# One column unit turned by transposing DMA, and one product's split in halves, in a Trainium2 kernel of 7803 matmuls

## The chip, the cores and the metric

The kernel runs on one core of one Trainium2 chip. A core has a matmul engine (TensorE, PE in the profile), three engines that work on vectors and elements (VectorE or DVE, ScalarE or ACT, GpSimd or POOL), an engine that here only issues transfers (SyncE or SP), and 16 DMA engines that carry the transfers. Each engine runs its own instructions in their order, and waits on semaphores for the others.

The metric is the device time of one execution in microseconds (us). Times are medians over runs. The profile shows one execution.

## The reference

One decoder layer on 256 tokens of width 2048, everything in float32: a feed-forward block, a token mixer of two branches, a second feed-forward block, and a last normalisation.

```python
def swiglu_ffn(x, w_gate, w_up, w_down):
    return (jax.nn.silu(x @ w_gate) * (x @ w_up)) @ w_down

x = x + 0.5 * swiglu_ffn(rms_norm(x, ffn1_norm), ffn1_w_gate, ffn1_w_up, ffn1_w_down)
z = rms_norm(x, mix_norm) @ w_in
...
x = x + y @ w_out
x = x + 0.5 * swiglu_ffn(rms_norm(x, ffn2_norm), ffn2_w_gate, ffn2_w_up, ffn2_w_down)
return rms_norm(x, final_norm)
```

Gate and up weights are 2048 x 5632, down weights 5632 x 2048. The change touches the first feed-forward block at its start, and the gate products of both blocks; the mixer (the lines left out) is not touched.

## The kernel before

**Numbers in two parts.** A float32 operand is split in two for TensorE: `hi`, which ACT makes as a copy rounded to the type fp32r, and `lo`, the remainder that DVE subtracts out. A product of two such operands is three matmuls: high by high, low of the tokens by high of the weights, high of the tokens by low of the weights. `multiply` (L231) issues the two terms with the weights' high part first, then the one with their low part; so `hi` is wanted first and `lo` eight matmuls per target bank later (two targets: sixteen). The tokens are the stationary operand, the weights stream in blocks of 128 x 512.

**Blocks of weights.** A block is one *unit* of four 128-row pieces and 512 columns, 1 MB, loaded by SP at L165 into one of three rotating buffers `raw` (or, for two special blocks of `seven`, into one of two buffers `kept`). A rotating buffer is loaded again only when all readers of its last content are done. ACT and DVE split each block, TensorE multiplies it. Everything is traced by a helper (L43), so that almost all instructions have this line; rows are told apart by the names of the tiles. A tile scheduler decides the order on each engine from the written order and its own model, except where instructions are kept in program order (`Engine.pinned`, `keep_in_program_order`).

**Seven products for eight.** `seven` (L405) computes two column blocks of gate, up or down weights at a time. On the first two row units (0 and 1) it takes the 2 x 2 blocks w11, w12, w21, w22 by a scheme with seven products in place of eight, in which sums of weights are multiplied by sums of tokens; units 2 and 3 (b2, b3 for the second column block, a2, a3 for the first) are multiplied the usual way. The order in the program is: product 0 (w11), product 4 (w12 - w11), b2, **product 5** (w22 less the last sum; the third product), b3, product 6 (w22 - w12), product 2 (w22), a2, product 3 (w21 less product 5's sum), a3, product 1 (w21). The names in rows are `hi_g_p`, `lo_g_p` for parts of products and `hi_g_x`, `lo_g_x` for usual blocks, `raw_g` for loaded blocks and the sums, which are made in place: w11 and then the sums of products 4, 5 and 3 stand in one buffer, w12 and then the sum of product 6 in another. With buffer numbers, `raw_g_2_00` is w11's, `_01` w12's, `_11` w22's, `_10` w21's, `_21` and `_31` b2's and b3's, `_20` and `_30` a2's and a3's. SP loads w11, w12, b2, w22, b3, a2, w21, a3 in this order; w21 goes into the rotating buffer that held b3, whose last reader is the DVE operation `lo_g_x` of b3.

The flag `order` is set for the third and fifth of the five gate calls of each feed-forward block: four calls in all, called gate blocks here. In these, the low halves of product 4 and the sum of product 6 keep their program order. In all calls the sum and the parts of product 4 are made in halves of two pieces each; product 5 has one full sum over 128 x 2048, two casts and one full low part.

**The opening.** `begin` starts the first feed-forward block while its inputs arrive. It is pinned to program order. The tokens, as loaded in `xres`, lie with tokens across the partitions and must be turned for TensorE, unit by unit. Unit u is first scaled by the tokens' factors (`tokens`: two ACT operations into `n`, one for each half of the tokens), then eight transposes on TensorE write it into four banks `pt` (`turned_tokens`), then ACT writes the high part (`high`: four operations that scale by the gain) and DVE the low part (`low`: four). For unit 3 the transposes are issued in the middle of the up product of unit 2. Between its low parts and the product stand, on ACT and DVE, the sums of tokens for `seven` (`steps`).

**Turning by DMA.** Elsewhere the kernel turns tiles without TensorE: `part` (L203) copies a 128 x 512 tile on ACT into a half of `pair`, with the two 16-bit halves of each float32 apart, and SP issues one transposing DMA (L208, 8 blocks of 128 x 128 16-bit numbers) back into the tile; `join` (L211) copies the turned halves on ACT into `pair` again, as float32.

Of the kernel before, what the change touches and what calls it, by code (L numbers as in the profile page):

```python
# [12 lines left out]
U16 = mybir.dt.uint16  # L13
AF = mybir.ActivationFunctionType
ALU = mybir.AluOpType
# [34 lines left out]
def hybrid_block(ctx: ExitStack, tc: tile.TileContext, a: dict, out: bass.AP):  # L50
# [35 lines left out]
    def f32(ap):  # L86
        return ap.bitcast(F32)
# [123 lines left out]
    def join(two, turned):  # L211
        tc.keep_in_program_order(act.copy(two.bitcast(U16).rearrange(mixed, b=2), turned.rearrange(flat, b=2)))
        return quad(two)
# [17 lines left out]
    def multiply(targets, blk, apart=False, middle=None):  # L231


        more = dict(skip_group_check=True) if apart else {}
        for ps, st, begin, _ in targets:
            for j in range(UK):
                pe.matmul(ps, st[j][0], blk[j][0], start=begin and j == 0, stop=False, **more)
                pe.matmul(ps, st[j][1], blk[j][0], start=False, stop=False, **more)
        if middle:
            middle()  # L240
        for ps, st, _, end in targets:
            for j in range(UK):
                pe.matmul(ps, st[j][0], blk[j][1], start=False, stop=end and j == UK - 1, **more)
        if len(targets) == NT:
            onward()
# [159 lines left out]
    def seven(w, rows, cols, sf, xs, name, keep, done, between=None, ready=None, whole=True, order=False):  # L405


        a, c, e, d = (bank(f"ps_{name}_{n}") for n in "aced")

        def get(u, n, kept=False):  # L410
            src = w[u * UK * P : (u + 1) * UK * P, cols[n] : cols[n] + CW]
            return load(src, f"{name}_{u}{n}", kept=kept)

        (r0, r1), two = rows, len(xs) > 1
        w11, first = ready or (get(r0, 0, True), None)
        w12 = get(r0, 1, True)
        b2, w22 = get(xs[0][0], 1), get(r1, 1)
        b3 = get(xs[1][0], 1) if two else None
        a2, w21 = get(xs[0][0], 0), get(r1, 0)
        a3 = get(xs[1][0], 0) if two else None  # L420

        def snap(ps, n):
            s = keep(f"{n}_{name}")
            act.copy(s, ps)
            return s

        def product_of(i, raw, ps, begin=False, end=True, blk=None):
            multiply([(ps, sf[i], begin, end)], blk or parts_of(raw, f"{name}_p{i}"), True)

        def usual(i, raw, n, *targets):  # L430

            blk = parts_of(raw, f"{name}_x{i}{n}")
            multiply([(ps, stationary(xs[i][1], t), b, z) for ps, t, b, z in targets], blk, True)

        product_of(0, w11, a, True, blk=first)
        s1 = None if whole else snap(a, "s1")
        if whole:
            act.copy(d, a)
        hi, lo, blk = splits_of(f"{name}_p4")
        for i in (0, 2):  # L440
            o = slice(i, i + 2)
            dve.tensor_tensor(w11[:, o], w12[:, o], w11[:, o], op=ALU.subtract)
            act.copy(hi[:, o], w11[:, o])
        for i in (0, 2):
            o = slice(i, i + 2)
            ins = dve.tensor_tensor(lo[:, o], w11[:, o], f32(hi[:, o]), op=ALU.subtract)
            if order:
                tc.keep_in_program_order(ins)
        product_of(4, w11, c, True, blk=blk)
        s5 = snap(c, "s5")  # L450
        if between:
            between(0)
        usual(0, b2, 1, (e, 1, True, not two), (c, 0, False, False))
        if between:
            between(1)
        dve.tensor_tensor(w11, w22, w11, op=ALU.subtract)
        product_of(5, w11, a)
        u2 = snap(a, "u2")
        if between:
            between(2)  # L460
        if two:
            usual(1, b3, 1, (e, 1, False, True), (c, 0, False, False))
        ins = dve.tensor_tensor(w12, w22, w12, op=ALU.subtract)
        if order:
            tc.keep_in_program_order(ins)
        product_of(6, w12, a)
        u3 = snap(a, "u3")
        done(1, 1, e, [u3, s5])
        product_of(2, w22, c)
        done(0, 1, c, [u2])  # L470
        usual(0, a2, 0, (d, 0, not whole, False), (a, 1, False, False))
        dve.tensor_tensor(w11, w21, w11, op=ALU.subtract)
        product_of(3, w11, a, end=not two)
        if two:
            usual(1, a3, 0, (a, 1, False, True), (d, 0, False, False))
        done(1, 0, a, [])
        product_of(1, w21, d)
        done(0, 0, d, [] if whole else [s1])

    def ffn(tag, norm, after, opening=False):  # L480
        with (
# [73 lines left out]
            def begin():  # L555
# [28 lines left out]
                def tokens(u):  # L584
                    n = [keep(f"n{tag}_{u}_{t}") for t in range(NT)]
                    for t in range(NT):
                        act.activation(n[t], xres[:, t, u * CW : (u + 1) * CW], AF.Copy, scale=norm.r[:, t : t + 1])
                    return n

                def turned_tokens(u, n):  # L590
                    pts = []
                    for j in range(UK):
                        pt = bank(f"pt{tag}_{u}_{j}")[:, :S]
                        for t in range(NT):
                            pe.transpose(pt[:, t * P : (t + 1) * P], n[t][:, j * P : (j + 1) * P], ident)
                        pts.append(pt)
                    return pts

                def high(u, pts):
                    for j, pt in enumerate(pts):  # L600
                        act.activation(units[u][:, j, :S], pt, AF.Copy, scale=gain[:, UK * u + j : UK * u + j + 1])

                def low(u, pts):
                    for j, pt in enumerate(pts):
                        g = gain[:, UK * u + j : UK * u + j + 1]
                        hi, lo = units[u][:, j, :S], units[u][:, j, S:]
                        dve.scalar_tensor_tensor(lo, pt, g, f32(hi), op0=ALU.mult, op1=ALU.subtract)

                def targets(banks, u, y):
                    return [(banks[t], stationary(y, t), u == 0, u in (0, 3)) for t in range(NT)]  # L610
# [52 lines left out]
                low(2, pts2)  # L663
                dve.tensor_tensor(lo, rg, f32(hi), op=ALU.subtract)
                raw["g", 3] = first_columns("g", 3)
                n3, pts3 = tokens(3), []
                multiply(targets(gps, 2, units[2]), blk, True)
                steps = []
                sums(steps)
                blk = parts("u", 2)  # L670
                raw["u", 3] = first_columns("u", 3)
                multiply(targets(ups, 2, units[2]), blk, True, middle=lambda: pts3.extend(turned_tokens(3, n3)))
                blk = parts("g", 3)
                steps[0]()
                high(3, pts3)
                low(3, pts3)
                steps[1]()
                multiply(targets(gps, 3, units[3]), blk, True)
                blk = parts("u", 3)
# [503 lines left out]
```

## Time and profile before

| | us |
|---|---|
| median of 3 runs | 1713.93 |
| lowest and highest run | 1713.70, 1714.16 |
| profiled execution | 1712.3 |
| its span, first to last instruction | 1710.3 |

Core 0 had a granted clock of 0.999 of full speed over the profiled execution. The span is what the profile divides into; the 2.0 us between it and the execution's time lie outside the first and the last instruction. A row of the timeline begins with its start and its length in us, then engine, line and operation, the output and the inputs, and the count of like instructions that it groups; a bracket gives the time for which the engine had been idle, and what released it. The start of a matmul row is what counts, since matmuls are pipelined and the length of a row is more than its share of the engine. DVE and ACT also let the next instruction begin a little before the end of the last.

### The profile page before, as it was taken

To read this page: it belongs to the slowest core of one execution; us is meant where nothing else is said; L and a number is where in the kernel's file an instruction comes from. 1 tells how busy PE (TensorE), PEld (TensorE's weight loads), DVE (VectorE), ACT (ScalarE), POOL (GpSimd) and SP (SyncE) were. 2 spreads that over 40 slices of the span, in tenths; PEclk is the share of its full clock that TensorE was granted. 3 is DMA by queue.
4 is the path that set the end of the run, shared out by engine and by line. 5 is a ranking of instruction groups with operands and counts; after the bars stand their busy time and mean duration, and the time that the engine had idled before them with its cause. 6 is when DMAs were issued, how large, how long until landed. Compare 5 with 4: busy or idle time off the path is not lost.

```text
span 1710.3 us, 20226 instructions
## 1 busy us (share of the span) xinstructions
PE 1693.9 (99%) x7803; PEld 1412.4 (83%) x7803; DVE 1480.0 (87%) x1297; ACT 1169.9 (68%) x1489; POOL 6.9 (0%) x32
## 2 busy tenths in 40 slices
PE   8999999999999999999999999999999999999997
PEld 6888888888888888888888888888888888888886
DVE  7998988979889879787986679979989888889786
ACT  6767667776567678775655777676667765677864
POOL 1000000000000000000000000000000000000000
PEclk9999999999999999999999999999999999999999
DMA  8666567575567685855555685685666656576753
GB/s 300 206 221 198 197 221 221 190 257 206 184 208 210 225 267 143 244 172 194 174 194 174 220 271 167 205 257 194 226 201 217 223 191 221 197 215 203 249 194 123
DMA packets 235168, 358.43 MB, mean 210 GB/s; under 512 B 66884, under 2 KB 69312, under 8 KB 234944
## 3 DMA queue, kind: packets, MB, share of 16 engines
q1 hardware_dynamic: 234608, 356.03, 64.7%
q8 instruction: 61, 1.00, 0.2%
q10 hardware_dynamic: 144, 1.05, 0.2%
q14 instruction: 35, 0.29, 0.1%
q0 software_dynamic: 320, 0.07, 0.0%
HBM read 339.82 MB, written 2.10 MB: 200 GB/s over the span
## 4 chain that ended last, share of the span: by engine, by line
PE 92%; ACT 3%; DVE 2%; DMA 1%; issue 1%; SPq 0%; DVEq 0%; ACTq 0%
PE ps_d L43 14%; PE ps_in L43 13%; PE ps_g_a L43 9%; PE ps_u_a L43 8%; PE ps_u_c L43 6%; PE ps_d_a L43 5%; PE ps_o L43 5%; PE ps_g_c L43 5%; PE ps_g_d L43 5%; PE ps_d_c L43 3%; PE ps_u_d L43 3%; PE ps_u_e L43 3%; PE ps_g_e L43 3%; PE ps_d_d L43 3%; PE ps_u L43 2%; PE ps_g L43 2%
## 5 line engine op out<-in xcount | busy, mean ns | idle before, releaser
L43 ACT CAST hi_u_p<-raw_u 128x1024 fp32r<-128x1024 f32 x140 | 141.5, 1047 | 52.5 <-DVE raw_u L43 24.7
L43 ACT CAST hi_g_p<-raw_g 128x1024 fp32r<-128x1024 f32 x132 | 133.8, 1047 | 57.6 <-DVE raw_g L43 30.2
L43 DVE TENSOR_TENSOR lo_u_p<-raw_u,hi_u_p 128x2048 fp32r<-128x2048 f32 (+1 forms) x80 | 159.9, 2018 | 14.4 <-ACT hi_u_p L43 13.8
L43 DVE TENSOR_TENSOR lo_g_p<-raw_g,hi_g_p 128x2048 fp32r<-128x2048 f32 (+1 forms) x75 | 151.6, 2030 | 18.7 <-ACT hi_g_p L43 17.9
L43 PE MATMUL ps_d<-hi_d,h 128*128 128x512 f32 x704 | 167.0, 389 | 0.0
L43 PEld LDWEIGHTS ps_d<-hi_d,h 128*128 128x128 f32 x704 | 132.2, 188 | 27.4
L43 PE MATMUL ps_in<-xT_nm,hi_in 128*128 128x512 f32 x640 | 153.1, 391 | 0.0
L43 PEld LDWEIGHTS ps_in<-xT_nm,hi_in 128*128 128x128 f32 x640 | 117.5, 188 | 23.0 <-ACT tha L43 0.3
L43 ACT CAST hi_d_p<-raw_d 128x1024 fp32r<-128x1024 f32 x84 | 86.1, 1048 | 65.7 <-DVE raw_d L43 34.2
L43 DVE TENSOR_TENSOR lo_d<-raw_d,hi_d 128x2048 fp32r<-128x2048 f32 x44 | 100.2, 2289 | 34.7 <-ACT hi_d L43 34.5
L43 ACT CAST hi_in<-raw_in 128x1024 fp32r<-128x1024 f32 x80 | 80.1, 1046 | 59.6 <-PE ps_in L43 46.2
L43 DVE TENSOR_TENSOR lo_in<-raw_in,hi_in 128x2048 fp32r<-128x2048 f32 x40 | 91.3, 2284 | 33.9 <-ACT hi_in L43 33.6
L43 ACT CAST hi_u_x<-raw_u 128x1024 fp32r<-128x1024 f32 x80 | 81.3, 1047 | 37.1 <-PE ps_u_c L43 25.9
L43 DVE TENSOR_TENSOR lo_d_p<-raw_d,hi_d_p 128x2048 fp32r<-128x2048 f32 (+1 forms) x48 | 96.4, 2019 | 7.2 <-ACT hi_d_p L43 6.8
L43 DVE TENSOR_TENSOR raw_u<-raw_u,raw_u 128x2048 f32<-128x2048 f32 (+1 forms) x50 | 92.3, 1862 | 11.2 <-DMA raw_u<-in_ffn_w_up_dram 10.6
L43 ACT CAST hi_d<-raw_d 128x1024 fp32r<-128x1024 f32 x88 | 88.8, 1046 | 18.0 <-PE ps_d_d L43 7.6
L43 DVE TENSOR_TENSOR lo_g_x<-raw_g,hi_g_x 128x2048 fp32r<-128x2048 f32 x40 | 91.4, 2286 | 7.5 <-ACT hi_g_x L43 7.5
L43 ACT CAST hi_g_x<-raw_g 128x1024 fp32r<-128x1024 f32 x80 | 81.2, 1046 | 20.4 <-PE ps_g_c L43 8.6
L43 DVE TENSOR_TENSOR lo_u_x<-raw_u,hi_u_x 128x2048 fp32r<-128x2048 f32 x40 | 91.3, 2283 | 1.2 <-ACT hi_u_x L43 1.1
L43 DVE TENSOR_TENSOR raw_g<-raw_g,raw_g 128x2048 f32<-128x2048 f32 (+1 forms) x46 | 84.9, 1867 | 5.4 <-DMA raw_g<-in_ffn_w_gate_dram 4.8
L43 PE MATMUL ps_d<-lo_d,h 128*128 128x512 f32 x352 | 87.3, 389 | 0.0
L43 PEld LDWEIGHTS ps_in<-xT_nm,lo_in 128*128 128x128 f32 x640 | 82.1, 191 | 3.1
(405 smaller groups left out, 3673.5 us busy)
## 6 DMA issues: line engine op xcount, KB each, us to landing
raw_d<-in_ffn_w_down_dram SPq DMA_DIRECT2D x88, 1024.0 KB, 5.7
raw_u<-in_ffn_w_up_dram SPq DMA_DIRECT2D x87, 1024.0 KB, 5.3
raw_g<-in_ffn_w_gate_dram SPq DMA_DIRECT2D x86, 1024.0 KB, 5.3
raw_in<-in_w_in_dram SPq DMA_DIRECT2D x40, 1024.0 KB, 5.1
raw_o<-in_w_out_dram SPq DMA_DIRECT2D x16, 1024.0 KB, 5.2
xres<-in_x_dram SPq DMA_DIRECT2D x4, 512.0 KB, 7.4
raw_u<-in_ffn_w_up_dram SPq DMA_DIRECT2D x2, 512.0 KB, 9.3
raw_g_first<-in_ffn_w_gate_dram SPq DMA_DIRECT2D x1, 1024.0 KB, 12.0
```

The costliest lines, as they stand in the source:

```text
L43: ins = getattr(self.engine, name)(*args, **kwargs)
```

## The change

Two edits. The first, in `begin`: unit 3 is no longer turned on TensorE. Each of its two tiles goes through `part` when it has been scaled (ahead of the gate product of unit 2), and through `join` after the split of the last gate weights, where `high` stood. `highs` then reads `pair` in four ACT operations with the gain, and the low parts are made by DVE from `pair`. The line `sides[0] = 1 - t` makes the first tile use one half of `pair` and the second the other, in a fixed order.

The second, in `seven` with the flag `order`: product 5's sum is made in two halves of 128 x 1024, each followed by its cast, and its low part in two halves.

```diff
@@ seven @@
-        dve.tensor_tensor(w11, w22, w11, op=ALU.subtract)
-        product_of(5, w11, a)
+        if order:
+            hi, lo, blk = splits_of(f"{name}_p5")
+            for i in (0, 2):
+                o = slice(i, i + 2)
+                dve.tensor_tensor(w11[:, o], w22[:, o], w11[:, o], op=ALU.subtract)
+                act.copy(hi[:, o], w11[:, o])
+            for i in (0, 2):
+                o = slice(i, i + 2)
+                dve.tensor_tensor(lo[:, o], w11[:, o], f32(hi[:, o]), op=ALU.subtract)
+            product_of(5, w11, a, blk=blk)
+        else:
+            dve.tensor_tensor(w11, w22, w11, op=ALU.subtract)
+            product_of(5, w11, a)
@@ begin @@
-                n3, pts3 = tokens(3), []
+                n3, planes = tokens(3), []
+                for t in range(NT):
+                    sides[0] = 1 - t
+                    planes.append(part(n3[t], n3[t].bitcast(U16)))
                 multiply(targets(gps, 2, units[2]), blk, True)
...
-                multiply(targets(ups, 2, units[2]), blk, True, middle=lambda: pts3.extend(turned_tokens(3, n3)))
+                multiply(targets(ups, 2, units[2]), blk, True)
                 blk = parts("g", 3)
                 steps[0]()
-                high(3, pts3)
-                low(3, pts3)
+                for t in range(NT):
+                    join(planes[t], n3[t].bitcast(U16))
+                gains = [gain[:, UK * 3 + j : UK * 3 + j + 1] for j in range(UK)]
+                views = [pair[:, :, j * P : (j + 1) * P] for j in range(UK)]
+                highs, lows = (
+                    [units[3][:, j, o : o + S].rearrange("p (t c) -> p t c", t=NT) for j in range(UK)] for o in (0, S)
+                )
+                for j in range(UK):
+                    act.activation(highs[j], views[j], AF.Copy, scale=gains[j])
+                for j in range(UK):
+                    dve.scalar_tensor_tensor(
+                        lows[j], views[j], gains[j], f32(highs[j]), op0=ALU.mult, op1=ALU.subtract
+                    )
                 steps[1]()
```

The order of ACT's instructions in the opening, before: the casts of the weights `hi_g` of unit 3, then the four scaled copies from the banks `pt` into `x_3`, the high part of unit 3, with the token sums `xs` behind them.

```order
L43 ACTIVATE n_3_0_401<-xres,r_n_213 128x512
L43 ACTIVATE n_3_1_402<-xres,r_n_213 128x512
L43 CAST xs_0_429<-spare_431 128x4x128
L43 CAST hi_u_0_2_435<-raw_u_0_2_328 128x1024 x2
L43 CAST hi_g_0_3_479<-raw_g_0_3_399 128x1024 x2
L43 ACTIVATE x_3_200<-pt_3_0_459,cols_first 128x256
L43 ACTIVATE x_3_200<-pt_3_1_462,cols_first 128x256
L43 ACTIVATE x_3_200<-pt_3_2_465,cols_first 128x256
L43 ACTIVATE x_3_200<-pt_3_3_468,cols_first 128x256
L43 CAST xs_0_429<-v_0_0_382 128x4x128
```

And now, with `pair<-n_3` of 128x1024 the copies of `part` and those of 128x2x512 the copies of `join`:

```order
L43 ACTIVATE n_3_0_401<-xres,r_n_213 128x512
L43 ACTIVATE n_3_1_402<-xres,r_n_213 128x512
L43 COPY pair<-n_3_0_401 128x1024
L43 COPY pair<-n_3_1_402 128x1024
L43 CAST xs_0_433<-spare_435 128x4x128
L43 CAST hi_u_0_2_439<-raw_u_0_2_328 128x1024 x2
L43 CAST hi_g_0_3_471<-raw_g_0_3_399 128x1024 x2
L43 COPY pair<-n_3_0_401 128x2x512
L43 COPY pair<-n_3_1_402 128x2x512
L43 ACTIVATE x_3_200<-pair,cols_first 128x256 x4
L43 CAST xs_0_433<-v_0_0_382 128x4x128
```

Two copies stand before the first token sum, and two after the casts of the last gate weights; the four scaled copies and what follows kept their order behind these.

SP's queue at the same place, now (before, the two DMA_TRANSPOSE rows were not there; the weights stood in the same order):

```order
L165 DMA raw_u_0_2_328<-in_ffn_w_up_dram 128x4x512
L165 DMA raw_g_0_3_399<-in_ffn_w_gate_dram 128x4x512
L208 DMA_TRANSPOSE n_3_0_401<-pair 128x8x128
L208 DMA_TRANSPOSE n_3_1_402<-pair 128x8x128
L165 DMA raw_u_0_3_445<-in_ffn_w_up_dram 128x4x512
L165 DMA raw_g_0_21_570<-in_ffn_w_gate_dram 128x4x512
```

The load of the last up weights (`raw_u_0_3`) stands behind both transposes.

DVE in a gate block (the third gate call of the first feed-forward block), before, from the first low half of product 4 to the low part of product 6; `h` and `z` belong to other work that the scheduler put in between:

```order
L43 TENSOR_TENSOR lo_g_2_p_2180<-raw_g_2_00_2145,hi_g_2_p_2179 128x1024
L43 TENSOR_TENSOR lo_g_2_x_2202<-raw_g_2_21_2149,hi_g_2_x_2201 128x2048
L43 TENSOR_TENSOR h_4_2116<-pair,h_4_2116 128x4x128
L43 TENSOR_TENSOR raw_g_2_00_2145<-raw_g_2_11_2151,raw_g_2_00_2145 128x2048
L43 TENSOR_TENSOR lo_g_2_x_2256<-raw_g_2_31_2153,hi_g_2_x_2255 128x2048
L43 TENSOR_TENSOR lo_g_2_p_2237<-raw_g_2_00_2145,hi_g_2_p_2236 128x2048
L43 TENSOR_TENSOR h_3_2284<-pair,h_3_2284 128x4x128
L43 TENSOR_TENSOR raw_g_2_01_2147<-raw_g_2_11_2151,raw_g_2_01_2147 128x2048
L43 TENSOR_TENSOR raw_g_2_00_2145<-raw_g_2_10_2157,raw_g_2_00_2145 128x2048
L43 TENSOR_TENSOR lo_g_2_p_2292<-raw_g_2_01_2147,hi_g_2_p_2291 128x2048
```

And now:

```order
L43 TENSOR_TENSOR raw_g_2_00_2139<-raw_g_2_11_2145,raw_g_2_00_2139 128x1024
L43 TENSOR_TENSOR lo_g_2_p_2174<-raw_g_2_00_2139,hi_g_2_p_2173 128x1024
L43 TENSOR_TENSOR lo_g_2_x_2196<-raw_g_2_21_2143,hi_g_2_x_2195 128x2048
L43 TENSOR_TENSOR h_4_2110<-pair,h_4_2110 128x4x128
L43 TENSOR_TENSOR raw_g_2_00_2139<-raw_g_2_11_2145,raw_g_2_00_2139 128x1024
L43 TENSOR_TENSOR lo_g_2_p_2230<-raw_g_2_00_2139,hi_g_2_p_2229 128x1024
L43 TENSOR_TENSOR lo_g_2_x_2252<-raw_g_2_31_2147,hi_g_2_x_2251 128x2048
L43 TENSOR_TENSOR lo_g_2_p_2230<-raw_g_2_00_2139,hi_g_2_p_2229 128x1024
L43 TENSOR_TENSOR h_3_2280<-pair,h_3_2280 128x4x128
L43 TENSOR_TENSOR raw_g_2_01_2141<-raw_g_2_11_2145,raw_g_2_01_2141 128x2048
L43 TENSOR_TENSOR raw_g_2_00_2139<-raw_g_2_10_2151,raw_g_2_00_2139 128x2048
L43 TENSOR_TENSOR lo_g_2_p_2288<-raw_g_2_01_2141,hi_g_2_p_2287 128x2048
```

The first half of product 5's sum moved ahead of product 4's second low half and of b2's low part. The second half of the sum and the first low half of product 5 stand ahead of b3's low part (`lo_g_2_x_2252`), and the second low half behind it; the sum of product 3 (with `raw_g_2_10`, w21) still stands ahead of product 6's low part.

## The prediction

> **What bounds the kernel now.** I read the page's header and chain of waits first, then the waits of TensorE alone, then the two places of the change in the timeline.
>
> ```profile
> span 1710.3 us, 20226 instructions
> ...
> PE 1693.9 (99%) x7803; PEld 1412.4 (83%) x7803; DVE 1480.0 (87%) x1297; ACT 1169.9 (68%) x1489; POOL 6.9 (0%) x32
> ...
> PE 92%; ACT 3%; DVE 2%; DMA 1%; issue 1%; SPq 0%; DVEq 0%; ACTq 0%
> ```
>
> TensorE (PE) is busy for 99% of the span and is 92% of the chain that ended last. So time is won in two ways only: fewer instructions on PE, or fewer waits of PE. All its waits are these five rows:
>
> ```profile
> PE pt_n L43 <- DMA xres<-in_x_dram: 3.0, 1, 3.0
> PE pv_first L43 <- DMA rows_first<-in_ffn_norm_dram: 2.6, 1, 2.6
> PE ps_g_a L43 <- DVE lo_g_p L43: 1.7, 4, 0.6
> PE ps_d_c L43 <- ACT s_d L43: 0.3, 1, 0.3
> PE ps_u L43 <- ACT hi_u_start L43: 0.2, 1, 0.2
> ```
>
> The third row is what the second half of the change is about: four waits, one in each gate block with the flag `order`, for the low part of product 5. The first half of the change takes eight transposes off PE in the opening. Nothing else can be won, so I size these two, and then look for what becomes late instead.
>
> **The opening.** The timeline of the stretch in which unit 3 of the input is turned:
>
> ```profile
> 33.08 1.37 ACT L43 ACTIVATE n<-xres,r_n 128x512 f32<-128x512 f32 x2
> ...
> 36.09 0.37 SPq L165 DMA_DIRECT2D raw_u<-in_ffn_w_up_dram  x1
> 36.66 0.62 ACT L43 CAST xs<-spare 128x512 fp32r<-128x512 f32 x1 [2.21 <-DVE spare L43]
> ...
> 39.08 1.99 ACT L43 CAST hi_g<-raw_g 128x1024 fp32r<-128x1024 f32 x2
> ...
> 39.34 3.80 PE L43 MATMUL ps_u<-hi_u,x 128*128 128x512 f32 x16
> ...
> 42.98 1.04 PE L43 MATMUL pt<-ident,n 128*128 128x128 f32 x8
> 43.40 1.57 ACT L43 ACTIVATE x<-pt,cols_first 128x256 fp32r<-128x256 f32 x4 [2.32 <-PE pt L43]
> ...
> 44.14 1.65 DVE L43 SCALAR_TENSOR_TENSOR x<-pt,cols_first,x 128x256 fp32r<-128x256 f32 x4
> ...
> 45.70 3.79 PE L43 MATMUL ps_g<-hi_g,x 128*128 128x512 f32 x16
> ...
> 48.15 1.99 ACT L43 CAST hi_u<-raw_u 128x1024 fp32r<-128x1024 f32 x2
> ```
>
> and the chain's row for the eight transposes:
>
> ```profile
> 43.14 0.88 PE pt L43 x8
> ```
>
> That row is the gain: eight transposes hold PE's chain for 0.88 us, 0.11 each. From 39.34 to 42.98 sixteen matmuls start, so one costs 0.2275 us; that step is used below.
>
> What replaces them: two copies into `pair`, two DMA transposes on SP, two joining copies. None of this is in this stretch before, but each stands elsewhere in the trace:
>
> ```profile
> L208 SPq DMA_TRANSPOSE z<-pair x17: 1232/1244/1252, 139.6 to 1621.0; - x17
> L43 ACT COPY pair<-xres x14: 1029/1040/1047, 647.9 to 1018.1; 128x1024 uint16<-128x1024 uint16 x14
> ...
> L43 ACT COPY pair<-cross_nm x6: 1342/1358/1366, 666.0 to 698.0; 128x1024 uint16<-128x1024 uint16 x6
> ...
> DMA to landing us min/median/max: 2.7/4.3/8.7
> ```
>
> ScalarE (ACT) is done with the two `n` at 34.45 and sat idle until 36.66; two copies of 1.04 fit into that gap, and end at about 36.4. SP then holds 1.24 us for each transpose: issued at 35.4 and 36.7, landed after 2.7 us (the quiet case) at 38.1 and 39.4, after the median 4.3 us at 39.7 and 41.0. ACT's `hi_g` ends at 41.07, the two joins of 1.36 follow, to 43.7; before, ACT waited there 2.32 us for PE. The four scaled copies then run 43.7 to 45.2, the first done at 44.1. PE, which now goes on without transposes, wants the first at 45.70 - 0.87 = 44.83 and its low part 0.23 later. VectorE (DVE) came to the low parts at 44.14, 0.7 after ACT's first scaled copy, and comes to them at the same time now. So nothing on PE waits, with 0.5 us and more in hand. Behind the transposes on SP stands the load of the last up weights, issued at 37.9 in place of 36.09; the load in the gate block below takes 5.78 us from issue to use, which gives 43.7, and ACT wants it at 48.15, so this is hidden.
>
> Bounds: at best the whole 0.88 us. At worst both transposes need the longest landing, 8.7 us: that is the slow rival below. Within the first gate block the scheduler now puts a half sum of DVE behind two operations that wait for PE's last opening product, and DVE has hardly a pause there, so I expect some tenths of new waits and take -0.7 us.
>
> The Trainium skill, "VectorE: DVE Perf Modes", section "The three transpose paths", speaks against this half: it gives 1309 ns for one 128x128 block by DMA against 390 ns on TensorE. If the eight blocks of each DMA transpose went one after the other, the second would land some 20 us late and the kernel would lose over 10 us. The trace does not agree: eight blocks landed after 2.7 to 8.7 us, and eight transposes on PE took 0.88 us, so I give that case no chance of its own.
>
> **The gate blocks.** One of the four in full (block 2 of the first FFN). Here `raw_g` is in turn w22 - (...) at 288.60, w22 - w12 before 298.90 and, at 298.90, the sum with w21:
>
> ```profile
> 283.90 0.69 DVE L43 TENSOR_TENSOR z<-ps_u_d,z 128x512 f32<-128x512 f32 x1
> ...
> 284.65 1.23 DVE L43 TENSOR_TENSOR lo_g_p<-raw_g,hi_g_p 128x1024 fp32r<-128x1024 f32 x1
> ...
> 288.00 0.69 DVE L43 TENSOR_TENSOR h<-pair,h 128x512 fp32r<-128x512 f32 x1
> ...
> 288.60 2.29 DVE L43 TENSOR_TENSOR raw_g<-raw_g,raw_g 128x2048 f32<-128x2048 f32 x1
> ...
> 290.80 2.29 DVE L43 TENSOR_TENSOR lo_g_x<-raw_g,hi_g_x 128x2048 fp32r<-128x2048 f32 x1
> ...
> 293.39 2.29 DVE L43 TENSOR_TENSOR lo_g_p<-raw_g,hi_g_p 128x2048 fp32r<-128x2048 f32 x1 [0.30 <-ACT hi_g_p L43]
> 293.43 1.98 PE L43 MATMUL ps_g_a<-hi_g_p,xs 128*128 128x512 f32 x8
> ...
> 295.73 1.20 PE L43 MATMUL ps_g_a<-lo_g_p,xs 128*128 128x512 f32 x4 [0.33 <-DVE lo_g_p L43]
> ...
> 298.90 2.29 DVE L43 TENSOR_TENSOR raw_g<-raw_g,raw_g 128x2048 f32<-128x2048 f32 x1 [0.41 <-DVE raw_g L43]
> ...
> 301.11 2.29 DVE L43 TENSOR_TENSOR lo_g_p<-raw_g,hi_g_p 128x2048 fp32r<-128x2048 f32 x1
> ```
>
> In the same stretch SP's row for the load of w21:
>
> ```profile
> 293.12 0.37 SPq L165 DMA_DIRECT2D raw_g<-in_ffn_w_gate_dram  x1
> ```
>
> What is lost now: PE could start the low part at 293.43 + 8 x 0.2275 = 295.25, and starts at 295.73, 0.48 late, and the restart costs some 0.1 more. So a wait of 0.33 costs about 0.6, and the four (1.7 us idle) cost 1.7 + 4 x 0.27 = 2.8 us, 2.7 with the spread of the rest. That is all this half can win.
>
> What the halves do: a full operation lets the next begin 2.20 us later (288.60 to 290.80), so a half of 1.23 us lets it begin 1.14 later; one of 128x512, 0.60 (288.00 to 288.60). In the new order DVE runs, from 283.90 + 0.61: half a sum (1.14), the low half of product 4 (1.14), a low part (2.20), `h` (0.60), half a sum (1.14), half a low part of product 5 (1.14), and only then `lo_g_x` of block b3, at 291.87. Its own length is 2.29, and then the second low half starts at 294.07 and ends at 295.30. PE wants that half at 293.43 + 10 x 0.2275 = 295.70. **The wait for product 5 goes**, in all four blocks.
>
> Where it goes: b3's low part began at 290.80 and now begins 1.07 us later. Its end frees the buffer into which w21 is loaded (before: ends 293.09, load issued 293.12). The sum with w21 stands on DVE ahead of product 6's low part, and already waited for this load, 0.41 us; three operations of DVE queue behind it. So product 6's low part comes 1.07 later, too. The other three blocks, where the sum with w21 is the second of the two (rows of PE and of DVE in turn):
>
> ```profile
> 542.06 1.98 PE L43 MATMUL ps_g_a<-hi_g_p,xs 128*128 128x512 f32 x8
> ...
> 544.86 4.48 DVE L43 TENSOR_TENSOR raw_g<-raw_g,raw_g 128x2048 f32<-128x2048 f32 x2
> ...
> 1297.34 1.97 PE L43 MATMUL ps_g_a<-hi_g_p,xs 128*128 128x512 f32 x8
> ...
> 1300.41 4.66 DVE L43 TENSOR_TENSOR raw_g<-raw_g,raw_g 128x2048 f32<-128x2048 f32 x2
> ...
> 1545.81 1.97 PE L43 MATMUL ps_g_a<-hi_g_p,xs 128*128 128x512 f32 x8
> ...
> 1548.59 4.53 DVE L43 TENSOR_TENSOR raw_g<-raw_g,raw_g 128x2048 f32<-128x2048 f32 x2
> ```
>
> Two sums back to back take 2.20 + 2.29 = 4.49; the pair at 1300.41 takes 4.66, so the load bounds it there, and at the other two it lands within 0.04 us of the time at which DVE is ready. The sums began at 298.90, 547.06, 1302.79 and 1550.84 (the pair's start and length less 2.29, to 0.01); with 1.07 added, product 6's low part is ready 2.21 + 2.29 later: at 304.47, 552.63, 1308.36, 1556.41. PE, no longer held at product 5, wants it 44 matmuls (10.01 us) after product 5's first: at 303.44, 552.07, 1307.35, 1555.82. It waits 1.03 + 0.56 + 1.01 + 0.59 = 3.2 us, with 0.12 a restart 3.7. Net of the 2.7 won, this half **costs 1.0 us**.
>
> Bounds: at best no wait at product 6, -2.7 us. The first load takes 298.90 - 293.12 = 5.78 us from issue to sum and held DVE up by 0.41; at worst the three others hold it up by 0.4 more each: +2.2 us. I take +1.0, the value of the blocks' own rows.
>
> By the Trainium skill, "VectorE: DVE Perf Modes", section "The TRN2 errata", each VectorE instruction pays a fixed cost beside its elements, some 150 cycles for such an fp32 operation, 0.16 us, so that one operation beats two halves. The rows agree in duration (2 x 1.23 - 2.29 = 0.17), while a back-to-back pair hides half of it. With the page's figure for both splits the four waits grow by some 0.2 each and the kernel by 0.8 us more.
>
> **Sum.** -0.7 + 1.0 = +0.3 us: a span of 1710.6 us. The profiled execution took 1712.3 us, its span and 2.0 around it, and the median of the runs shown is 1713.93, 1.6 above that; forecast **1714.2 us**.
>
> **The rivals.** *The gate blocks pay in full* (15%): product 6 does not wait, because the load of w21 lands early enough. For it: at two blocks the sum with w21 began without a visible wait. Against: there the load landed just then, and it is issued by the same end of `lo_g_x`. Time 1713.93 - 0.7 - 2.7 = 1710.5.
>
> *Only the opening pays* (14%): the wait at product 6 equals the one removed, for it takes only 0.25 us less in each block. Time 1713.2.
>
> *Slower, by the landing of the transposes* (12%). Place: ACT's two joins, ahead of the scaled copies, `xs` and `hi_u` on an in-order engine. With 8.7 us the second lands at 45.4 and is joined at 46.8, where ACT began the scaled copies at 43.40 before: 3.4 us late. PE waits for the first from 44.83 to 47.2, and ACT and DVE, with no pauses to catch up in, are 3.4 late in the next products: 3.4 us on top of the forecast, 1717.6. It decides from a landing of some 6.4 us on (second transpose after 43.1). For it: the weights are streamed on the same queue. Against: by 35.4 only one load is still on its way.
>
> *The change as said, with other work put late by the new order* is inside the forecast's own range, 1713.0 to 1715.8 (59%).
>
> 0.2% of this time, 3.4 us, is about what a measurement tells from no change. Faster than 1710.5: half of the first rival and a remainder of the others, 10%. Slower than 1717.4: most of the slow rival and a little of the forecast's upper tail, 11%. Within: 79%. The range that leaves out some 2 in 10 reaches into both: 1710.7 to 1716.8.
>
> **What would show it.** Right: PE's waits have no `ps_g_a` for `lo_g_p` between 295 and 296 any more but four of 0.3 to 0.9 us some 8 us later, in front of product 6's low part; the load of w21 issued 1 us later against PE; the transposes of `n` landed before 41 and no PE wait at `ps_g` near 45. Wrong: no wait at product 6 (the first rival), or ACT idle before the joins (the slow one). A new wait of PE anywhere else over 1 us would mean that the order moved something that I took as covered.

## The result

The change made the kernel slower. Medians on the chip: 1723.07 us (1716.74 to 1725.61, 8 runs) against 1714.17 us before (1713.20 to 1716.04, 8 runs); the ratio is 1.0046, 95% interval 1.0036 to 1.0056. The forecast was 1714.2 us, with a range of 1710.7 to 1716.8. Besides the 9 us, the runs now spread over 9 us where they spread over 3.

The profiled execution took 1719.71 us, less than the median. Its page and TensorE's waits answer to the first two fences of the prediction:

```profile
span 1717.9 us, 20228 instructions
...
PE 1696.3 (99%) x7795; PEld 1410.6 (82%) x7795; DVE 1480.9 (86%) x1305; ACT 1173.7 (68%) x1493; POOL 6.9 (0%) x32
```

```profile
...
PE ps_d_c L43 <- ACT s_d L43: 2.4, 2, 2.1
PE ps_g_a L43 <- DVE lo_g_p L43: 1.8, 5, 0.5
PE ps_g_c L43 <- ACT s_g L43: 1.8, 4, 0.6
PE ps_u_a L43 <- DVE lo_u_p L43: 1.0, 2, 0.8
...
```

TensorE has eight instructions fewer and is still busy for 99%, but four groups of waits stand where one of 1.7 us stood. The second row has the name of the old wait and is another one: four of its five stand at product 6 (below), one of 0.30 in a gate block without the flag. Rows three and four were not there, and the first was 0.3.

**The opening** came out as worked out in the prediction. The rows of the same stretch now:

```profile
35.39 2.68 SPq L208 DMA_TRANSPOSE n<-pair  x2
...
39.32 3.79 PE L43 MATMUL ps_u<-hi_u,x 128*128 128x512 f32 x16
...
40.96 2.58 ACT L43 COPY pair<-n 128x1024 uint16<-128x1024 uint16 x2
...
43.57 1.71 ACT L43 ACTIVATE x<-pair,cols_first 128x256 fp32r<-128x256 f32 x4
44.12 1.69 DVE L43 SCALAR_TENSOR_TENSOR x<-pair,cols_first,x 128x256 fp32r<-128x256 f32 x4
44.76 3.79 PE L43 MATMUL ps_g<-hi_g,x 128*128 128x512 f32 x16
```

Their landing, in the list of transfers (count, median us from issue):

```profile
n<-pair SPq DMA_TRANSPOSE x2, 2.8
```

The joins begin when `hi_g` is done, with no idle time ahead of them; the last gate product of the opening begins at 44.76, not at 45.70, and waits for nothing. From the first matmul with `hi_u_start` to the first of the first gate block (`ps_g_a`) TensorE has the same order in all kernels of this document, but for the eight transposes; this stretch took 42.3 to 42.5 us in the three traces with the old opening and 40.8 to 41.6 us in the eleven with the new one.

**A gate block**, the same one as in the prediction (rows of the timeline of the change):

```profile
287.20 1.05 ACT L43 CAST hi_g_p<-raw_g 128x1024 fp32r<-128x1024 f32 x1
...
288.15 1.05 ACT L43 CAST hi_g_x<-raw_g 128x1024 fp32r<-128x1024 f32 x1
...
289.10 0.58 ACT L43 COPY s_g<-ps_g_c 128x512 f32<-128x512 f32 x1
...
289.73 2.12 PE L43 MATMUL ps_g_c<-hi_g_x,x 128*128 128x512 f32 x8 [0.34 <-ACT s_g L43]
...
293.51 1.98 PE L43 MATMUL ps_g_a<-hi_g_p,xs 128*128 128x512 f32 x8
...
295.33 1.07 PE L43 MATMUL ps_g_a<-lo_g_p,xs 128*128 128x512 f32 x4
...
299.53 2.29 DVE L43 TENSOR_TENSOR raw_g<-raw_g,raw_g 128x2048 f32<-128x2048 f32 x1 [2.02 <-DMA raw_g<-in_ffn_w_gate_dram]
...
301.74 4.49 DVE L43 TENSOR_TENSOR lo_g_p<-raw_g,hi_g_p 128x2048 fp32r<-128x2048 f32 x2
...
304.08 1.20 PE L43 MATMUL ps_g_a<-lo_g_p,xs 128*128 128x512 f32 x4 [0.43 <-DVE lo_g_p L43]
```

Three things are to be seen. Product 5's low part follows its high part without a wait (295.33 is eight matmuls behind 293.51): the old wait has gone. The wait at 304.08 is in front of product 6's low part, because DVE stood 2.02 us at 299.53 for the load of w21: the forecast's new wait. And the wait at 289.73 was not in the forecast: the b2 product's second half goes into bank c, which must first be copied out to `s_g` by ACT, and ACT has a cast of product 5 (287.20) ahead of that copy. Before, the copy ended ahead of the matmuls that need the bank:

```profile
287.77 1.04 ACT L43 CAST hi_g_x<-raw_g 128x1024 fp32r<-128x1024 f32 x1
...
288.72 0.57 ACT L43 COPY s_g<-ps_g_c 128x512 f32<-128x512 f32 x1
...
289.80 1.98 PE L43 MATMUL ps_g_c<-hi_g_x,x 128*128 128x512 f32 x8
```

**The last down block**, in the chain of waits of the change (start, length, what):

```profile
1633.59 8.29 DMA fin<-in_final_norm_dram
1641.91 0.43 DVE fin L43
...
1664.08 0.49 ACT s_d L43
1664.62 2.11 PE ps_d_c L43 x8
```

The chain of the kernel before was TensorE alone in this stretch. Now it passes through a load of the last norm's gains and DVE's scaling of them. DVE's row there, of the change and, behind it, of before:

```profile
1641.91 0.43 DVE L43 TENSOR_SCALAR fin<-fin 128x512 f32<-128x512 f32 x1 [4.20 <-DMA fin<-in_final_norm_dram]
```

```profile
1635.82 0.43 DVE L43 TENSOR_SCALAR fin<-fin 128x512 f32<-128x512 f32 x1 [1.31 <-DMA fin<-in_final_norm_dram]
```

DVE stands 4.20 us there instead of 1.31. The diff does not touch this line; the scheduler moved it. Before, three operations stood ahead of it that now stand behind: a low part `lo_d` (128x2048) and two sums of 128x512 (`z`, `u_g`). DVE thus comes to it earlier, and the load has not landed.

The load itself is issued by ACT, and ACT had stood at a transposing DMA of the hidden tokens a little earlier. Rows of ACT in the change:

```profile
1628.44 2.27 ACT L43 COPY pair<-z 128x1024 uint16<-128x1024 uint16 x2 [1.71 <-DMA z<-pair]
...
1633.59 0.38 ACTq L1126 DMA_DIRECT2D fin<-in_final_norm_dram  x1
```

In the kernel before, ACT does not stand there. So how late the gains come hangs on the landing of that transpose too, and ACT's stand differs between executions of one kernel (1.71 us here, 3.11 in the second trace of the change, below).

The table adds up TensorE's lost time by place: each distance between the starts of two matmuls, less the usual 0.227 us (0.12 and 0.11 for narrower ones), for places with 0.15 us or more; restarts are in it. The last four columns are kernels of the next section. Each column is one execution. Smaller losses at other places, 0.4 to 1.5 us in all in each column, are left out.

| us lost by TensorE | before | change | e3_snap | e5_both | e10_best | e11_snapcost |
|---|---|---|---|---|---|---|
| gate blocks: b2 into bank c (`s_g`), four | 0 | 2.92 | 0 | 0 | 0 | 2.69 |
| gate blocks: product 5's low part, four | 2.74 | 0 | 0 | 0 | 0 | 0 |
| gate blocks: product 6's low part, four | 0 | 2.63 | 4.70 | 0 | 0 | 0 |
| gate blocks: product 2's low part, four | 0 | 0 | 0 | 3.73 | 0 | 0 |
| up blocks behind them: product 5's low part | 0 | 1.97 | 2.30 | 0.72 | 1.56 | 0 |
| last down block (`s_d`) | 0 | 2.38 | 0.24 | 0 | 0 | 0 |
| down block ahead of the mixer (`s_d`) | 0.53 | 0.53 | 2.26 | 0.53 | 0.53 | 0.52 |

### The profile page after: what moved, and what is told of

It is laid out like the page before. It is cut to its first block, busy times and chain, and to the rows that moved or that the text cites. A ratio compares the mean times of both kernels' runs of the same rounds, so it can differ in the third digit from the quotient of the medians.

```text
span 1717.9 us, 20228 instructions
## 1 busy us (share of the span) xinstructions
PE 1696.3 (99%) x7795; PEld 1410.6 (82%) x7795; DVE 1480.9 (86%) x1305; ACT 1173.7 (68%) x1493; POOL 6.9 (0%) x32
## 5 line engine op out<-in xcount | busy, mean ns | idle before, releaser
L43 DVE TENSOR_TENSOR raw_g<-raw_g,raw_g 128x1024 f32<-128x1024 f32 (+1 forms) x50 | 85.7, 1734 | 13.0 <-DMA raw_g<-in_ffn_w_gate_dram 13.0
```

The costliest lines, as they stand in the source:

```text
L43: ins = getattr(self.engine, name)(*args, **kwargs)
```

## The experiments

Two theories stood against each other at first. Mine: the halves in the gate blocks cost everything, by ACT's order, by the load of w21 and by what becomes late behind them. The rival: the transposing DMAs, and the order that the scheduler makes behind them, cost it. The kernel before ran beside each group, at medians of 1713.4 to 1713.9 us.

**e1_opening** keeps only the opening's half:

```diff
-        if order:
-            hi, lo, blk = splits_of(f"{name}_p5")
...
-        else:
-            dve.tensor_tensor(w11, w22, w11, op=ALU.subtract)
-            product_of(5, w11, a)
+        dve.tensor_tensor(w11, w22, w11, op=ALU.subtract)
+        product_of(5, w11, a)
```

> The opening's half alone; product 5 is made as before, in full. My theory (the halves in the gate blocks are what costs): the 0.88 us of PE transposes goes, a few tenths come back in the first gate block, and no wait over 0.3 us appears anywhere else; 0.5 to 0.9 us under the kernel before, with its small spread from run to run. The rival (the DMA transposes at the start and the order that the scheduler makes behind them carry the loss): 5 to 9 us over the kernel before, runs spread over several us, and the wait of PE for s_d in the last down block is there.

1713.41 us (1712.24 to 1714.07, 11 runs) against 1713.88; ratio 0.9999, interval 0.9990 to 1.0008. By the medians the gain of 0.5 us is inside the interval; the stretch of the opening (40.8 us, 42.5 before; the change 41.5) shows it. No new wait over 0.3 us follows but one of 0.48 us in the first down block. The rival falls.

**e2_halves** keeps only the halves (the diff's first part on the kernel before).

> The halves alone; unit 3 is turned on PE as before. My theory: the two new waits in each gate block (bank c for the copy s_g on ACT, 0.6 to 0.9 us, and product 6's low part, 0.6 to 0.75) are there in all four, with the waits in the up blocks and the last down block behind them; 8 to 10 us over the kernel before, and spread over several us. The rival: 1 to 2 us over the kernel before at most, with no wait in the last down block.

1721.58 us (1719.71 to 1722.69, 5 runs); ratio 1.0045, interval 1.0033 to 1.0058. Its waits are those of the change, and one more in an up block behind a gate block without the flag (the last row):

```profile
PE ps_d_c L43 <- ACT s_d L43: 2.6, 2, 2.3
...
PE ps_g_c L43 <- ACT s_g L43: 1.6, 4, 0.6
PE ps_g_a L43 <- DVE lo_g_p L43: 1.3, 4, 0.4
PE ps_u_a L43 <- DVE lo_u_p L43: 1.1, 2, 0.8
PE ps_u_c L43 <- DVE lo_u_p L43: 0.9, 1, 0.9
```

The loss is in the halves; the spread of 3 us was smaller than I expected.

**e3_snap** is the change, with product 5's casts held behind the copy `s_g`:

```diff
-            act.copy(s, ps)
+            snaps[n] = act.copy(s, ps)
...
-                act.copy(hi[:, o], w11[:, o])
+                with tc.issue_after(snaps["s5"].ins):
+                    act.copy(hi[:, o], w11[:, o])
```

> The change whole, with product 5's two casts on ACT kept behind the copy s_g. If the first cast, put ahead of s_g, makes PE's four waits before the b2 product into bank c: these 2.9 us go, the waits at product 6's low part grow by up to 0.6 each since PE comes there earlier and the load of w21 does not; together 0.5 to 3 us under the change, 1720 to 1722.5. If s_g is late for another reason (PE's own low part of product 4, DVE), the four waits stay and the time is that of the change, 1723.

1718.02 us (1715.87 to 1720.15, 11 runs). The four waits for `s_g` are gone, and those at product 6's low part grew from 2.63 to 4.70 us in all (table), as expected. The median fell by 5.1 us (between two groups), more than the 3 expected. One reason is that with this edit the scheduler also put the scaling of the gains back behind the three operations, as before, and the loss in the last down block fell to 0.24. Against that, the kept trace has a wait of 2.0 us for `s_d` in another place, the down block ahead of the mixer, where the change waits 0.3:

```profile
PE ps_d_c L43 <- ACT s_d L43: 2.0, 1, 2.0
```

```profile
623.90 2.25 ACT L43 COPY pair<-z 128x1024 uint16<-128x1024 uint16 x2 [3.92 <-DMA z<-pair]
```

Some 30 us earlier ACT had stood 3.92 us for a transposing DMA of the hidden tokens (1.02 in the change), and DVE behind it 3.49 us for ACT (0.61 in the change). So this run alone does not price `s_g`.

**e5_both** also puts the sum with w21 behind product 6's low part on DVE:

```diff
+            lo6 = dve.tensor_tensor(lo, w12, f32(hi), op=ALU.subtract)
+            with tc.issue_after(lo6.ins):
+                dve.tensor_tensor(w11, w21, w11, op=ALU.subtract)
...
-        dve.tensor_tensor(w11, w21, w11, op=ALU.subtract)
+        if not order:
+            dve.tensor_tensor(w11, w21, w11, op=ALU.subtract)
         product_of(3, w11, a, end=not two)
```

> As the last one, and in the gate blocks product 6's low part stands ahead of the sum with w21 on DVE. If the load of w21, through that sum, holds product 6's low part: the four waits there go too, DVE has no backlog into the up blocks, and the time is 1710.5 to 1713, under the kernel before. If the tail's wait and the spread come from the opening, or from the higher count of DVE instructions, it stays at 1717 or more.

1714.49 us (1713.85 to 1715.27, 11 runs), between the two expectations. The waits at product 6 are gone, and four others stand one product further on:

```profile
PE ps_g_c L43 <- DVE lo_g_p L43: 2.7, 4, 0.8
```

This is product 2's low part, which now stands behind the sum. The sum of 2.2 us seems to make late what stands behind it; the next run tries this.

**e7_behind2** moves the sum once more, behind product 2's low part:

```diff
+            with tc.issue_after(lo6.ins):
+                lo2 = dve.tensor_tensor(lo, w22, f32(hi), op=ALU.subtract)
+            with tc.issue_after(lo2.ins):
+                dve.tensor_tensor(w11, w21, w11, op=ALU.subtract)
```

> As e5_both, with the sum with w21 one place further back on DVE in the gate blocks, behind product 2's low part. In e5_both PE's four waits had moved there (0.89, 0.87, 1.09 and 0.88 us with restarts, 3.7 in all). If it is this sum of 2.2 us that makes whatever stands behind it late: they go, none comes at b2's or a2's low part, nor at product 3, and the time is 1710.5 to 1711.5. If DVE as a whole is too late there (two more instructions, 87% busy), the waits move on again to a2's or product 3's low part and the time stays at 1714 to 1715.

1711.50 us (1710.22 to 1713.07, 11 runs) against 1713.83; ratio 0.9987, interval 0.9978 to 0.9996. The waits did not move on: none is left at product 2, a2 or product 3. DVE has time for this sum there, since TensorE comes to product 3 only after product 2 and a2.

**e8_fin** is the change with one DVE instruction held at its written place:

```diff
-                    dve.tensor_scalar(lastgain, lastgain, -0.5, None, op0=ALU.mult)
+                    tc.keep_in_program_order(dve.tensor_scalar(lastgain, lastgain, -0.5, None, op0=ALU.mult))
```

All other instructions stand in the same order on every engine as in the change.

> The change whole; the only difference is the place of one DVE instruction in the last down block, which scales a quarter of the last norm's gains: from 45 places ahead of their use to right ahead of it. If the wait of PE for s_d (2.4 us in the change's trace), and much of the spread from run to run, come from DVE standing 4.2 us at this instruction until the gains are loaded: that wait falls under 0.6 us, the median to 1718 to 1721, the spread to under 5 us. If it comes from a backlog out of the gate and up blocks before, the wait stays and so does the median, 1723.

1717.32 us (1716.38 to 1722.18, 7 runs): 5.75 under the change's median in another group of runs, more than expected; one run lies far from the others. The wait has its old size:

```profile
PE ps_d_c L43 <- ACT s_d L43: 0.3, 1, 0.3
```

So the place of one instruction that the diff does not name carries a large part of the loss. The two kept traces differ by 1.0 us only: the change's was one of its short executions, and of it 2.4 us were lost in the last down block.

**e9_nosnap** is e7_behind2 without the edit for `s_g`.

> As e7_behind2, but product 5's first cast stands ahead of the copy s_g on ACT again, as in the change. If the four waits for s_g are a cost of their own: 2.4 to 3.2 us over e7_behind2, at the four b2 products into bank c, and as much as the last down block waits besides. If they only hid a wait that comes later anyway, it is within 1 us of e7_behind2.

1716.97 us (1713.52 to 1719.83, 11 runs), 5.5 over e7_behind2, with the scaling of the gains at the change's place again. That is more than the 2.4 to 3.2 expected for `s_g`, and the last down block, which was to add the rest, has no wait in the kept trace. Its waits for `s_g` are there (2.1 us by the profile's list, four). Two causes are mixed in this difference; the next runs try to part them.

**e10_best** is e7_behind2 with e8_fin's edit, **e11_snapcost** is e9_nosnap with it:

> As e7_behind2, with the scaling of the gains at its use, as in e8_fin. In e7_behind2 this instruction stands where it stood before the change, so little should follow: 1710.5 to 1711.5, at most 0.6 us from e7_behind2. If even at the old place DVE's stand at it was worth something, 1 us or more under e7_behind2.

> As e9_nosnap (first cast of product 5 ahead of the copy s_g), with the scaling of the gains at its use. If e9_nosnap's 5.5 us over e7_behind2, and its spread of 6 us, are the four waits for s_g (2.9) and DVE's stand at the gains: 2.4 to 3.3 us over e10_best, with a spread of 4 us or less. If the gains have no part in it: 5 us over e10_best, spread as before.

e10_best: 1711.30 us (1709.87 to 1712.67, 11 runs) against 1713.82; ratio 0.9987, interval 0.9978 to 0.9996. e11_snapcost: 1712.66 us (1711.70 to 1713.86, 11 runs). Between e9_nosnap and e11_snapcost only the place of the scaling of the gains differs: 4.3 us by the medians (of two groups), and a spread of 6.3 us that becomes 2.2. But the kept trace of e9_nosnap does not show this cost. DVE stands there as in the change,

```profile
1638.23 0.43 DVE L43 TENSOR_SCALAR fin<-fin 128x512 f32<-128x512 f32 x1 [3.29 <-DMA fin<-in_final_norm_dram]
```

and yet TensorE has no wait for it. All kernels with the new opening issue their matmuls in one order, so their traces can be laid side by side matmul by matmul: this one ends 3.9 us behind that of e11_snapcost, of which 2.7 are lost at product 4 and the product behind it (534 to 542 us) and only 0.25 in the last down block. How much of the 4.3 us belongs to the gains is therefore open.

Between e11_snapcost and e10_best ACT's order at `s_g` differs, and two neighbours on DVE in the last down block changed places: 1.36 us, less than the 2.4 to 3.3 expected. The table shows where it goes: e11_snapcost loses 2.69 us at `s_g` and nothing in the up blocks behind, e10_best loses nothing at `s_g` and 1.56 in the up blocks. That TensorE's wait gives DVE time to catch up would explain it; no run tested it.

**e12_noopening** is e10_best with unit 3 turned on TensorE (the diff's second part taken back).

> As e10_best, with unit 3 turned by TensorE as before the change. The opening's half alone was worth 0.5 us by the medians (e1_opening) and 0.88 by the chain's row: 0.4 to 0.9 us over e10_best. If the DMA transposes hold up the weights behind them and cost as much as they save, equal or under e10_best.

1711.96 us (1711.05 to 1713.79, 11 runs): 0.66 over e10_best, as expected, though small against the spread of either kernel (2.7 and 2.8 us). The opening's half is worth about this much.

**e13_change** and **e14_fin** are the change and e8_fin once more, side by side.

> The change itself once more, beside the next kernel on the same chip, because the trace shows 2.4 us at the last down block and the medians of different calls 5.75. If the gains' place costs what the medians say: 1721 to 1725, 5 us or more over the next kernel. If the difference of the calls was chance: 1719 to 1721, 2 to 3 us over it.

> The same as e8_fin, beside the change: 1716.5 to 1718.5, with no wait over 0.6 us for s_d in the last down block.

1723.48 us (1720.06 to 1725.23, 5 runs) and 1719.02 us (1717.80 to 1720.26, 6 runs): 4.5 us, between what the two theories said, and e14_fin lies 0.5 over its expectation. Its trace has one wait of 1.3 us for `s_d` in the down block ahead of the mixer, again behind a stand of ACT (3.40 us) for a transposing DMA. The profiled execution of the change now took 1725.23 us and shows a longer wait in the last down block:

```profile
1663.77 1.97 PE L43 MATMUL ps_d_e<-hi_d_x,h 128*128 128x512 f32 x8
1668.49 2.83 PE L43 MATMUL ps_d_c<-hi_d_x,h 128*128 128x512 f32 x8 [2.75 <-ACT s_d L43]
1671.12 1.91 PE L43 MATMUL ps_d_e<-lo_d_x,h 128*128 128x512 f32 x4
```

By the starts, 3.0 us are lost at 1668.49, and 1.5 more in the matmuls behind it. That is 4.5 together, the difference of the medians; but it is one execution, the longest of the five, and it lost another 2.2 us at product 4 of one gate block. ACT's row ahead of the load of the gains is here

```profile
1633.06 2.26 ACT L43 COPY pair<-z 128x1024 uint16<-128x1024 uint16 x2 [3.11 <-DMA z<-pair]
```

In the four traces with the gains at the early place, ACT stood there 1.27 us (e9_nosnap), 1.71 (the change), 2.48 (e2_halves) and 3.11 (e13_change), and TensorE then waited for nothing, 2.11, 2.30 and 2.75 us. The two go together; no run held one fixed.

## Why the prediction was wrong

**Opening, -0.7: right.** The transposes landed after 2.8 us, the quiet case, no load behind them came late, and the expected tenths of new waits stand in the first gate block (0.17 and 0.19 us by the starts). Measured: -0.5 by the medians of e1_opening (not clear of noise), -0.66 by e12_noopening. The case that the prediction drew from the Trainium skill ("VectorE: DVE Perf Modes", section "The three transpose paths") would have shown as a landing some 20 us late; it did not come.

**Product 5's wait goes, -2.7: right.** The row is empty in every kernel with the halves.

**Product 6's low part waits instead, +3.7: right in mechanism, place and about in size.** With TensorE not held before (e3_snap) the four waits are 4.70 us against 3.7 worked out: at the two blocks for which I let the load bind least, 1.11 and 1.10 us against 0.68 and 0.71 with the restart, since in all four blocks DVE stands 1.7 to 1.9 us at the load. (The rows of the kernel before gave for these two blocks only the latest time at which the load could have landed, and the prediction took it as the time itself.) In the change itself DVE stands there for 1.9 to 2.1 us, and the four waits are 2.63 in all, since TensorE, held at `s_g`, comes 0.6 to 0.9 later to each. What I left out is the up block behind: 1.97 us more, which I put down to this stand of DVE, of 2.02 us where it was 0.41 in the block shown. It cannot be the stand alone, since e10_best, with the sum moved back, still loses 1.56 there. Between e8_fin and e11_snapcost, which differ in the place of the sum with w21 and in what the scheduler moved around it, lie 4.7 us by the medians (of two groups).

**The first step that failed: "where the wait goes" was followed on DVE and SP, not on ACT.** The half sum at 283.94, ahead of b2's low part, makes a cast ready for ACT; I counted it as time won for product 5 and never asked what stands behind it on ACT. It is the copy that frees bank c. Four waits of 0.6 to 0.9 us; 1.4 us net when what they hide is counted (e11_snapcost against e10_best).

**The second: what the new order moves elsewhere was put into the forecast's range as "other work put late", without looking at those places.** The prediction named a new wait over 1 us anywhere else as the sign of this, and that is what came: waits of 2.1 to 2.75 us in the last down block, from an instruction three places earlier on DVE, ahead of a load that had not landed. By the medians this instruction's place costs 4.5 to 5.8 us, by the traces 2.4 (the change), 4.5 (e13_change) or next to nothing (e9_nosnap). The forecast's own range had 1.6 us of room for it.

By the medians, e10_best with its 1711.30 and the change are apart by ACT's order (+1.36), the sum with w21 (+4.66) and the gains' place (+5.75 to the change's first median; e13_change and e14_fin, side by side, give +4.46). These three are steps from one kernel to the next, so that they end at the change's 1723.07 is no test of them. The traces are one: matmul by matmul, the change's first execution ends 8.4 us behind e10_best's, and the rows of the table account for that with 2.9 at `s_g`, 2.6 at product 6, 0.4 more in the up blocks and 2.4 in the last down block. The three edits together take the loss away, and that is shown; the share of each differs between the executions that were traced and the medians. Without the three costs it would have gone nearly as the rival "the gate blocks pay in full" had it, at 1710.5 us; e10_best has 1711.30.

**The slow rival** had the right side and the wrong place: the joins on ACT waited for nothing.

What stays open: in some executions (e7_behind2, e9_nosnap, e13_change, one gate block each) the trace shows about 2.2 us lost at product 4, some 10 us after ACT had stood 1.9 to 2.7 us for a transposing DMA of the hidden tokens. The wait in the down block ahead of the mixer (e3_snap, e14_fin) and the late load of the gains follow such a stand too. No run took this apart; it can hide in any of the medians. Nor was the scaling of the gains tried at the early place in the kernel before, so whether it costs anything without the backlog of the gate blocks was not shown.

## What to carry to other kernels

Where a scheduler sets the order, an edit that makes one operation ready earlier changes the order of each engine that works for it. Read the whole difference, engine by engine, and for every instruction that moved ahead of others ask what it waits for and who stands behind it; an instruction on a busy in-order engine that is early and depends on a load is a risk, even where its result is wanted much later. Splitting an operation pays when what stands between the halves, and what waits on a load behind them, is placed too: the same halves cost 7.7 us in the order that came by itself (e2_halves), and won 1.9 us (ratio 0.9990, interval 0.9981 to 0.9999) with the casts, the sum with w21 and the scaling held in place (e12_noopening). And where executions of one kernel differ by several us, one trace shows where time can be lost, and not how much of the median is lost there.

## What the runs showed of the hardware

The granted clock of TensorE fell behind two of the waits in the last down block, and not behind a third that was little shorter. Rows of the view of stretches (the third number from the end is the clock granted, as a share of full speed): the change's first trace, with 2.11 us idle at 1664.62,

```profile
1664.40:1668.40 4.00, 3.78 (x17) 3.14 (x18) 4.00 (x6) 4.00 (x8) 0.00 (x0) 1.00 0.48 186
```

e2_halves, with 2.30 us idle at 1665.20,

```profile
1664.80:1668.80 4.00, 3.60 (x9) 2.83 (x10) 4.00 (x6) 3.47 (x7) 0.00 (x0) 0.57 0.55 212
```

and e13_change, with 2.75 us idle at 1668.49:

```profile
1668.20:1672.60 4.40, 4.11 (x12) 3.25 (x13) 4.40 (x6) 4.40 (x9) 0.00 (x0) 0.66 0.45 173
1672.60:1677.00 4.40, 4.40 (x20) 3.62 (x19) 3.88 (x3) 1.97 (x3) 0.00 (x0) 0.95 0.46 143
```

In e2_halves and in e13_change the matmuls behind the wait lost 1.5 us more by their starts, within about 4 us; in the first trace of the change none. So in these executions a wait of 2.30 us cost 1.5 us more than one of 2.11. In e2_halves the wide steps begin with the first matmul behind the wait, in e13_change only with the fifth, so the length of the wait need not be all that decides; three cases do not give a threshold. This can be one reason for which the last down block's wait costs more by the medians than in the first trace. The Trainium skill, "TensorE: Matmul & The Clock Gate", section "Part 1: The HAM clock gate", puts the fall at an idle window of some 3.4 us; these traces show it after a wait of 2.30.
